# The PSUM pool of the down products in a decoder layer: two double banks, or four single ones

## The chip, the cores and the metric

The kernel runs on one core of a Trainium2 chip. The metric is the device time of one execution in microseconds. Five engines work from queues of their own: PE (TensorE, matmuls; its weight loads appear as PEld), DVE (VectorE, called V in the code), ACT (ScalarE, A), POOL (GpSimd, G) and SP (SyncE, which issues the DMAs here). Each takes its instructions in the order in which they stand in its queue, and engines wait for each other through semaphores. The sums of matmuls arise in PSUM; in this program a PSUM bank holds 512 f32 numbers for each of the 128 partitions, and eight banks are shared out by two pools.

## The reference, cut to what matters

The program is one whole decoder layer; the change lies in its second half, the feed-forward part, where 1024 tokens of width 1024 go through gate, up and down products with an inner width of 2816:

```python
def swiglu(h, w_gate, w_up, w_down):
    return (jax.nn.silu(h @ w_gate) * (h @ w_up)) @ w_down

h = x * (1.0 + scale2) + shift2
ffn = swiglu(h, w_gate[l], w_up[l], w_down[l])
x = layer_norm(ALPHA * x + gate2 * ffn, ln2_g[l], ln2_b[l])
```

## The kernel before

**Stages.** Modulation, projections, token index, attention and the output projection with the first layer norm take the first part of the program; the feed-forward part follows. It cuts the inner width of 2816 into 11 parts of 256 (`NFP`). For each part there is a gate product, an up product and a down product. All three use seven block products in place of eight (a Strassen scheme), with sums and differences of blocks; so a part has seven gate steps, seven up steps and seven down steps. In this text g0 to g6, u0 to u6 and d0 to d6 are these steps. For each part p from 1 to 9, the string `DOWN_AT` (L60) sets their order: g0 g1 d0 g2 d1 g3 d2 g4 d3 g5 d4 g6 d5 u0 d6 u1 u2 u3 u4 u5 u6, where the d steps belong to the part before. One such pass is called a round here. There are nine rounds; parts 9 and 10 get their down products after them, in the tail, by another loop.

**Steps.** A g or u step (`gu_step`, L1376) is 12 matmuls of 128x512 into one single bank of the pool `ps1` (u3 is cut in two halves of 6, the second behind u4). A d step (`down_step`, L1545) is also 12 matmuls: four groups of tokens, i = 0 to 3, with three matmuls each, into a bank for each group, b0 to b3. DVE then adds (or subtracts) each bank to a 512-wide half of a residual tile `res_X`, one instruction for each bank; these are called the reads of b0 to b3. Steps d0, d2, d4 and d6 begin a new sum (new tiles from the pool); d1, d3 and d5 add to the sum that stands in the bank, after DVE has read the partial sum once.

**PSUM before.** The pool `ps1` has four single banks, `ps2` has two tiles of two banks each. A new down sum takes both tiles of `ps2`: b0 and b1 are the halves of one, b2 and b3 of the other. The tile framework puts in the waits: a write to a tile waits for the reads of that tile that stand ahead of it in the program.

**Weights.** f32 precision is kept by splitting every operand in a rounded high part and a low rest, with three matmuls for a product. `make_block` (L1322) does it for a block of weights: where the scheme wants a sum or difference, POOL forms it in the raw weights first (`wraw`; for down weights POOL also multiplies by the gate); ACT writes the high half of the block (`wblk`, "the ACT half"); then DVE (gate and up) or POOL (down) writes the low half. There are four block buffers, and each step's end asks for the block that is needed four steps later, in the buffer that this step has just used. So on ACT, POOL and DVE the making of blocks stands in between the other work of the steps. Raw weights of a whole product (1 MB) have two buffers; the DMA for the next but one product is issued when the last block of a product is made.

**Order.** In the nine rounds PE, DVE, ACT and POOL run in the order of the program (`pinned`, L1564), with nothing reordered. After a g or u step's evacuation, the next lines of the program are the block (ACT half, DVE half), and then the d step with its reads. So DVE does the low half of a block for a gate or up step right ahead of the reads of the next d step.

The name `L159` in the profile is the helper through which all compute instructions go; the groups are told apart by their tiles: `gu` (gate and up sums), `dn` (down sums), `res_X`, `wblk`, `wraw`, `act` (activations split in two halves), `gtmp` and `utmp` (their intermediate sums).

Of the kernel before, what the change touches and what calls it, by code (L numbers as in the profile page):

```python
# [171 lines left out]
def decoder_layer_kernel(  # L172
# [16 lines left out]
        area[nm_] = at  # L189
        at += 4 * words  # L190
    nc.alloc_sbuf_tensor("arena", [P, (at - nc.sbuf_base) // 4], F32)
    ps2 = ctx.enter_context(tc.tile_pool(name="ps2", bufs=2, space=bass.MemoryType.PSUM))
    ps1 = ctx.enter_context(tc.tile_pool(name="ps1", bufs=4, space=bass.MemoryType.PSUM))

    def buf(where, off, n, name, dt=F32):
        return nc.alloc_sbuf_tensor_at(f"{name}_{where}{off}", [P, n], dt, offset=area[where] + 4 * off).ap()

    n_ps = [0]

    ps_ring = {"ps1": [], "ps2": []}  # L200

    def ps_tile(pool, tag, n, depth, nm):
        n_ps[0] += 1
        t = pool.tile([P, n], F32, tag=tag, name=f"{nm}_{n_ps[0]}")
        ring = ps_ring[tag]
        times.prev[t[:, 0:n].name] = ring[-depth] if len(ring) >= depth else None
        ring.append(t[:, 0:n].name)
        return t
# [4 lines left out]
    def psB(nm="pb"):  # L213
        return ps_tile(ps2, "ps2", 1024, 2, nm)
# [725 lines left out]
    for n_, (kind, a, b) in enumerate(groups):  # L940
        if n_ in PAIRS:
            pb = psB("pair")
# [184 lines left out]
    for n_, u in enumerate(units):  # L1127
        g, pr, i = u
# [178 lines left out]
    def block(n):  # L1307
        if n < 7:
            return FIRST[n]
        if n < len(blocks) - 8 or n >= len(blocks) - 4:  # L1310
            return RING[(n - 7) % NRING]
        return TOK[:, 1, n + 8 - len(blocks)]
# [50 lines left out]
    def use_blocks(n):  # L1363
        pos["used"] += n

        lead = LEAD + 4 if pos["used"] >= len(blocks) - 11 else LEAD
        while pos["made"] < min(pos["used"] + lead, len(blocks)):
            make_block()
# [76 lines left out]
    def after_step():  # L1445

        for f in low:
            f()
        low[:], low2[:] = low2, []

    def gate_up(kind, act, after=None):
        for n in range(7):
            gu_step(kind, n, 0, 4, act)
            if after is not None:
                after(n)
# [63 lines left out]
    def E(rc, i):  # L1519

        t = 7 - 2 * i if rc >= 20 else 6 - 2 * i
        return XR[t][:, 0:512] if rc % 10 == 1 else XR[t][:, 512:1024]
# [3 lines left out]
    def affine(n=0):  # L1526
        if todo:
            t = todo.pop(0)
            V.tensor_tensor(XR[t], XR[t], GR, ALU.mult)
            (G if t in AFF_G else V).tensor_tensor(XR[t], XR[t], lnb, ALU.add)  # L1530
            if t % 2 == 0:
                for to in (12, 21):
                    G.tensor_tensor(E(to, (7 - t) // 2), E(to, (7 - t) // 2), E(22, (7 - t) // 2), ALU.subtract)
            if not todo:
                SP.dma_start(GR, g2_d.to_broadcast([P, 1024]))
# [4 lines left out]
            affine()  # L1540
    gate_up("u", ACTS, lambda n: affine())

    bank = {}

    def down_step(p, n):  # L1545
        a_, w_, new, (to,) = DOWN[n]
        wd_ = block(pos["used"])
        if new:
            pb = [psB("dn"), psB("dn")]
            bank.update({i: pb[i // 2][:, (i % 2) * 512 : (i % 2 + 1) * 512] for i in range(4)})  # L1550
        for i in range(4):
            for m, (a, b) in enumerate(SPLITS):
                T.matmul(bank[i], ACTS[a_][:, a * 512 + i * P : a * 512 + (i + 1) * P], wd_[:, b * 512 : (b + 1) * 512],
                         start=(new and m == 0), stop=(m == 2), skip_group_check=True)
            z = E(abs(to), i)
            op = ALU.add if to > 0 else ALU.subtract
            if p == 0 and (n == 0 or not new):
                V.scalar_tensor_tensor(z, z, float(np.float32(ALPHA)), bank[i], ALU.mult, op)
            else:
                V.tensor_tensor(z, z, bank[i], op)  # L1560
        use_blocks(1)
        after_step()

    pinned.update("TVAG")  # L1564
    for p in range(1, NFP - 1):
        n_of = {"g": 0, "d": 0, "u": 0}
        for kind in DOWN_AT:
            n = n_of[kind]
            n_of[kind] += 1
            if kind == "d":  # L1570
                down_step(p - 1, n)
            else:
                gu_step(kind, n, 0, 4, None if kind == "g" else ACTS if p < NFP - 2 else PLAIN, kind == "u")
# [110 lines left out]
```

## Time and profile before

| | |
|---|---|
| median of 3 runs | 1800.81 us (1799.05 to 1803.73) |
| the profiled execution | 1800.09 us |
| its span on the engines | 1798.1 us, 15974 instructions |
| DVE busy | 1033.1 us (57%) |
| ACT busy | 607.8 us (34%) |
| POOL busy | 785.2 us (44%) |
| PE with d steps, by window | 106.0 us from 1056 to 1162: PE 71.82 us, DVE 40.32, ACT 22.05, POOL 38.03 busy |

How to read it: a row of the timeline gives the start of an instruction (or of a run of like ones) from the span's start, its duration, the engine, the operation with the tiles that it writes and reads, the count, and in brackets the idle time of the engine just before with what ended it. Rows of windows give the busy time of PE, PEld, DVE, ACT and POOL with counts in a stretch, the granted TensorE clock as a share of the full one, and the DMA's share and rate.

### The profile page before, as it was taken

The numbers are of one execution on the slowest core, as the hardware profiler recorded it, in microseconds if no ns is written. First come the engines' busy times: TensorE is split into PE (matmuls) and PEld (weight loads), VectorE is DVE, ScalarE is ACT, GpSimd is POOL, SyncE is SP. The second block draws the span as 40 slices with busy tenths as digits, with TensorE's granted clock in tenths as the row PEclk, the third lists the DMA queues.
The fourth block names the chain that finished last, engine by engine and source line by source line (L and its number), as shares of the span: only waits on it lengthen the run. The fifth ranks groups of instructions, "written<-read, shape, count | busy, mean of one in ns | idle before, by whom it ended". The sixth has DMA issues, their size and how long they took to land.

```text
span 1798.1 us, 15974 instructions
## 1 busy us (share of the span) xinstructions
PE 1348.8 (75%) x5462; PEld 1001.1 (56%) x5462; DVE 1033.1 (57%) x1740; ACT 607.8 (34%) x1141; POOL 785.2 (44%) x764
## 2 busy tenths in 40 slices
PE   8889786869979967676676857678576775766797
PEld 6655665645647866454454645456355553544576
DVE  7998989997784885333343333434333343333468
ACT  3556254656764552112121121212112122121231
POOL 1647576634453365615224161431614225162437
PEclk9999898878989988787886887878787797877999
DMA  9400120100464011010100101001010010101012
GB/s 352 165 36 30 53 101 17 59 18 13 146 224 153 1 36 59 0 47 24 47 24 24 47 1 47 23 24 47 1 47 24 24 47 9 61 2 47 24 71 94
DMA packets 24999, 101.80 MB, mean 57 GB/s; under 512 B 3411, under 2 KB 3411, under 8 KB 20566
## 3 DMA queue, kind: packets, MB, share of 16 engines
q1 hardware_dynamic: 24918, 100.78, 15.9%
q8 instruction: 43, 0.70, 0.2%
q14 instruction: 38, 0.31, 0.1%
HBM read 92.38 MB, written 8.40 MB: 56 GB/s over the span
## 4 chain that ended last, share of the span: by engine, by line
PE 29%; DVE 13%; POOL 7%; ACT 6%; issue 4%; DVEq 0%; ACTq 0%; POOLq 0%
PE gu L159 16%; PE dn L159 14%; DVE res_X L159 6%; POOL wraw_R L159 2%; DVE gtmp_V L159 2%; ACT wblk_V L159 2%; ACT wblk_T L159 2%; POOL wraw_W L159 1%; ACT gtmp_V L159 1%; POOL gtmp_V L159 1%; DVE wblk_V L159 1%; DVE wblk_T L159 1%; DVE act_W L159 1%; ACT act_W L159 1%; POOL act_W L159 1%
## 5 line engine op out<-in xcount | busy, mean ns | idle before, releaser
L159 DVE TENSOR_TENSOR res_X<-res_X,dn 128x512 f32<-128x512 f32 (+1 forms) x253 | 172.7, 683 | 179.9 <-PE dn L159 179.6
L159 PE MATMUL gu<-hr_H,wblk_V 128*128 128x512 f32 (+1 forms) x936 | 244.6, 417 | 18.0 <-POOL hr_H L159 11.7
L159 PE MATMUL gu<-hr_H,wblk_T 128*128 128x512 f32 (+1 forms) x924 | 247.3, 426 | 6.8 <-ACT gtmp_V L159 4.4
L159 PEld LDWEIGHTS gu<-hr_H,wblk_V 128*128 128x128 f32 x936 | 193.5, 211 | 62.2 <-POOL hr_H L159 12.3
L159 PE MATMUL dn<-wblk_V,act_W 128*128 128x512 f32 x324 | 122.5, 509 | 140.9 <-DVE res_X L159 123.8
L159 PEld LDWEIGHTS gu<-hr_H,wblk_T 128*128 128x128 f32 x924 | 197.4, 218 | 52.5 <-ACT gtmp_V L159 4.8
L159 PE MATMUL dn<-wblk_T,act_W 128*128 128x512 f32 x324 | 120.8, 504 | 136.8 <-DVE res_X L159 119.1
L159 PEld LDWEIGHTS dn<-wblk_V,act_W 128*128 128x128 f32 x324 | 70.7, 235 | 185.2 <-DVE res_X L159 152.7
L159 PEld LDWEIGHTS dn<-wblk_T,act_W 128*128 128x128 f32 x324 | 69.6, 231 | 180.1 <-DVE res_X L159 147.6
L159 POOL TENSOR_TENSOR wraw_R<-wraw_R 128x512 f32<-128x512 f32 x64 | 85.8, 1344 | 152.2 <-DVE wblk_V L159 81.2
L159 POOL TENSOR_TENSOR wraw_W<-wraw_W 128x512 f32<-128x512 f32 x60 | 78.6, 1315 | 135.1 <-DVE wblk_T L159 68.8
L159 PE MATMUL pj<-ws_W,hT_H 128*128 128x512 f32 x456 | 124.3, 421 | 17.8 <-ACT pout_K L159 5.4
L159 PEld LDWEIGHTS pj<-ws_W,hT_H 128*128 128x128 f32 x456 | 88.6, 201 | 45.4 <-issue 15.0
L159 ACT ACTIVATE wblk_V<-wraw_R 128x512 fp32r<-128x512 f32 x56 | 35.1, 627 | 166.0 <-PE dn L159 107.3
L159 POOL TENSOR_SCALAR sm_H<-sm_H,stat_X 128x1024 f32<-128x1024 f32 (+7 forms) x64 | 58.3, 924 | 71.2 <-DVE stat_X L159 58.2
L159 DVE TENSOR_TENSOR wblk_V<-wraw_W,wblk_V 128x512 fp32r<-128x512 f32 x40 | 31.2, 780 | 90.2 <-ACT wblk_V L159 89.8
L159 DVE TENSOR_TENSOR wblk_T<-wraw_W,wblk_T 128x512 fp32r<-128x512 f32 x41 | 31.3, 764 | 85.5 <-ACT wblk_T L159 85.3
L159 DVE TENSOR_TENSOR wblk_V<-wraw_R,wblk_V 128x512 fp32r<-128x512 f32 x38 | 29.8, 784 | 87.8 <-ACT wblk_V L159 84.3
L159 DVE TENSOR_SCALAR_CACHE_REDUCE junk_X<-keysD_T,colsD_X 128x1024 int16<-128x1024 int16 (+1 forms) x64 | 78.9, 1270 | 0.8
L159 ACT ACTIVATE wblk_T<-wraw_R 128x512 fp32r<-128x512 f32 x53 | 33.0, 625 | 128.3 <-PE dn L159 93.2
L159 ACT ACTIVATE wblk_T<-wraw_W 128x512 fp32r<-128x512 f32 x55 | 34.3, 625 | 123.0 <-PE dn L159 87.3
L159 ACT ACTIVATE wblk_V<-wraw_W 128x512 fp32r<-128x512 f32 x54 | 33.8, 626 | 124.0 <-PE dn L159 83.5
(299 smaller groups left out, 2805.4 us busy)
## 6 DMA issues: line engine op xcount, KB each, us to landing
wm_K<-in_wma_dram SPq DMA_DIRECT2D x16, 512.0 KB, 10.0
modraw_V<-in_wmc_dram SPq DMA_DIRECT2D x16, 512.0 KB, 4.3
wraw_R<-in_wg_dram SPq DMA_DIRECT2D x6, 1024.0 KB, 4.8
wraw_R<-in_wd_dram SPq DMA_DIRECT2D x6, 1024.0 KB, 4.8
wraw_W<-in_wup_dram SPq DMA_DIRECT2D x6, 1024.0 KB, 4.7
modraw_V<-in_wmg_dram SPq DMA_DIRECT2D x10, 512.0 KB, 4.6
wraw_R<-in_wup_dram SPq DMA_DIRECT2D x5, 1024.0 KB, 4.7
wraw_W<-in_wg_dram SPq DMA_DIRECT2D x5, 1024.0 KB, 4.8
```

The lines of the kernel that those rows point to most:

```text
L159: ins_ = f(*a, **k)
```

## The change

The pool of the double banks is closed when the last up product ahead of the rounds is written, and a third pool, `ps3`, of four single banks takes its place. A new down sum takes four single tiles of it. To let a pool be closed ahead of the others, `ps1` is now opened first, so the two pools lie the other way round in PSUM. Matmuls, reads, blocks, loads and their order are the same.

```diff
-    ps2 = ctx.enter_context(tc.tile_pool(name="ps2", bufs=2, space=bass.MemoryType.PSUM))
     ps1 = ctx.enter_context(tc.tile_pool(name="ps1", bufs=4, space=bass.MemoryType.PSUM))
+    pairs = ExitStack()
+    ps2 = pairs.enter_context(tc.tile_pool(name="ps2", bufs=2, space=bass.MemoryType.PSUM))
...
-    ps_ring = {"ps1": [], "ps2": []}
+    ps_ring = {"ps1": [], "ps2": [], "ps3": []}
...
     gate_up("u", ACTS, lambda n: affine())
 
+    pairs.close()
+    ps3 = ctx.enter_context(tc.tile_pool(name="ps3", bufs=4, space=bass.MemoryType.PSUM))
     bank = {}
 
     def down_step(p, n):
         a_, w_, new, (to,) = DOWN[n]
         wd_ = block(pos["used"])
         if new:
-            pb = [psB("dn"), psB("dn")]
-            bank.update({i: pb[i // 2][:, (i % 2) * 512 : (i % 2 + 1) * 512] for i in range(4)})
+            bank.update({i: ps_tile(ps3, "ps3", 512, 4, "dn") for i in range(4)})
```

On PE, the place is step d1 of the second round, where a sum that stands in the banks is added to. Before, `dn_5676` is the double bank of b0 and b1, and `dn_5677` that of b2 and b3:

```order
L159 MATMUL dn_5676<-wblk_V_4094,act_W_4105 128x512 [waits Activation_49]
L159 MATMUL dn_5676<-wblk_V_4094,act_W_4105 128x512 [waits Pool_49]
L159 MATMUL dn_5676<-wblk_V_4094,act_W_4105 128x512
L159 MATMUL dn_5676<-wblk_V_4094,act_W_4105 128x512 [waits DVE_49]
L159 MATMUL dn_5676<-wblk_V_4094,act_W_4105 128x512 x2
L159 MATMUL dn_5677<-wblk_V_4094,act_W_4105 128x512 x3
L159 MATMUL dn_5677<-wblk_V_4094,act_W_4105 128x512 [waits DVE_49]
L159 MATMUL dn_5677<-wblk_V_4094,act_W_4105 128x512 x2
```

The same step in the changed kernel, where `dn_5688` to `dn_5691` are the four single banks:

```order
L159 MATMUL dn_5688<-wblk_V_4094,act_W_4105 128x512 [waits DVE_49,Activation_49]
L159 MATMUL dn_5688<-wblk_V_4094,act_W_4105 128x512 [waits Pool_49]
L159 MATMUL dn_5688<-wblk_V_4094,act_W_4105 128x512
L159 MATMUL dn_5689<-wblk_V_4094,act_W_4105 128x512 [waits DVE_49]
L159 MATMUL dn_5689<-wblk_V_4094,act_W_4105 128x512 x2
L159 MATMUL dn_5690<-wblk_V_4094,act_W_4105 128x512 [waits DVE_49]
L159 MATMUL dn_5690<-wblk_V_4094,act_W_4105 128x512 x2
L159 MATMUL dn_5691<-wblk_V_4094,act_W_4105 128x512 [waits DVE_49]
L159 MATMUL dn_5691<-wblk_V_4094,act_W_4105 128x512 x2
```

Before, the write of b1 waits for DVE, and that of b3. Since both banks of a pair are one tile, the wait ahead of b1 is for the read of b0 in this same step. In the changed kernel each bank waits for DVE once, for the read of this bank in the step before; the waits for ACT and POOL (the block's two halves) are where they were.

On DVE, the order of instructions around the same step, before:

```order
L159 TENSOR_TENSOR wblk_T_4097<-wraw_R_4101,wblk_T_4097 128x512 [waits PE_49,Activation_49]
L159 TENSOR_TENSOR res_X_4079<-res_X_4079,dn_5676 128x512 [waits PE_49]
L159 TENSOR_TENSOR res_X_4077<-res_X_4077,dn_5676 128x512 [waits PE_49]
L159 TENSOR_TENSOR res_X_4075<-res_X_4075,dn_5677 128x512 [waits PE_49]
L159 TENSOR_TENSOR res_X_4073<-res_X_4073,dn_5677 128x512 [waits PE_49]
```

And in the changed kernel:

```order
L159 TENSOR_TENSOR wblk_T_4097<-wraw_R_4101,wblk_T_4097 128x512 [waits PE_49,Activation_49]
L159 TENSOR_TENSOR res_X_4079<-res_X_4079,dn_5688 128x512 [waits PE_49]
L159 TENSOR_TENSOR res_X_4077<-res_X_4077,dn_5689 128x512 [waits PE_49]
L159 TENSOR_TENSOR res_X_4075<-res_X_4075,dn_5690 128x512 [waits PE_49]
L159 TENSOR_TENSOR res_X_4073<-res_X_4073,dn_5691 128x512 [waits PE_49]
```

Nothing moved on DVE: the low half of the block still stands ahead of the four reads, and it waits for ACT. Only the tiles that the reads name are others.

## The prediction

> **What bounds the kernel now.** I read the page first (busy shares), then the list of waits, then the windows and the timeline of one round of the feed-forward part.
>
> ```profile
> PE 1348.8 (75%) x5462; PEld 1001.1 (56%) x5462; DVE 1033.1 (57%) x1740; ACT 607.8 (34%) x1141; POOL 785.2 (44%) x764
> PE dn L159 <- DVE res_X L159: 269.2, 126, 10.8
> ACT wblk_V L159 <- PE dn L159: 190.8, 32, 7.1
> ```
>
> No engine is full. The largest wait between PE and another engine is 269.2 us in 126 waits: a matmul of a down step waits for DVE to read a bank. Nine rounds of seven steps are 63 steps, so it is two waits a step: the writes of b1 and b3, which the order rows show waiting for the read of the other half of their pair. ACT in turn waits for PE to finish the step, since its block buffer is free only then. So the engines take turns.
>
> The windows show what this does to the clock, the timeline what it does to one step (d0 of the fifth round):
>
> ```profile
> 1166.50:1182.00 15.50, 12.04 (x33) 8.46 (x34) 4.73 (x7) 1.75 (x3) 9.62 (x8) 0.71 0.01 1
> 1132.00:1142.00 10.00, 10.00 (x46) 8.28 (x45) 3.93 (x6) 2.77 (x5) 0.00 (x0) 1.00 0.31 105
> 1165.78 0.67 DVE L159 TENSOR_TENSOR res_X<-res_X,dn 128x512 f32<-128x512 f32 x1
> 1166.51 2.93 PE L159 MATMUL dn<-wblk_V,act_W 128*128 128x512 f32 x6 [10.00 <-DVE res_X L159]
> 1168.20 0.69 DVE L159 TENSOR_TENSOR res_X<-res_X,dn 128x512 f32<-128x512 f32 x1 [1.74 <-PE dn L159]
> 1170.22 1.65 PE L159 MATMUL dn<-wblk_V,act_W 128*128 128x512 f32 x3 [0.78 <-DVE res_X L159]
> 1171.67 4.73 PE L159 MATMUL gu<-hr_H,wblk_T 128*128 128x512 f32 x12
> 1248.58 5.40 PEld L159 LDWEIGHTS gu<-hr_H,wblk_T 128*128 128x128 f32 x24
> ```
>
> PE stands 10.00 us before b1, until the read of b0 (1165.78) is done, writes b1 and b2 together, stands 0.78 us before b3. DVE in its turn waits 1.74 us for b1. Among these waits the granted clock is 0.71, and 12 matmuls take 4.73 us (0.39 us each); in the dense stretch of up steps it is 1.00, and 24 weight loads take 5.40 us (0.225 us for a load with its matmul).
>
> How long a round is, and where its up part ends, read from the first read of d0 (rounds 1, 6 and 9 here, round 5 above) and from ACT's copy of u4 (rounds 5 and 9), which starts when u4 is done:
>
> ```profile
> 733.14 0.68 DVE L159 SCALAR_TENSOR_TENSOR res_X<-res_X,dn 128x512 f32<-128x512 f32 x1
> 1275.25 0.67 DVE L159 TENSOR_TENSOR res_X<-res_X,dn 128x512 f32<-128x512 f32 x1
> 1599.27 0.67 DVE L159 TENSOR_TENSOR res_X<-res_X,dn 128x512 f32<-128x512 f32 x1
> 1247.64 0.60 ACT L159 ACTIVATE utmp_X<-gu 128x512 f32<-128x512 f32 x1 [2.96 <-PE gu L159]
> 1680.22 0.60 ACT L159 ACTIVATE utmp_X<-gu 128x512 f32<-128x512 f32 x1 [2.96 <-PE gu L159]
> ```
>
> Mean round: (1599.27 - 733.14) / 8 = **108.27 us**. In round 5 the part from d0's read to u4's end is 1247.64 - 1165.78 = 81.86 us, and from there to the next read of d0 27.61 us; in round 9 the first part is 80.95 us.
>
> **The change, part by part.** The two pools' places in PSUM, and closing one ahead of the rounds, add no instruction on any engine: nothing, and the stages ahead cost what they did. No matmul, read, block or DMA is added or moved. What goes are the 126 waits for the other half of a pair. What comes is a wait of each bank for its own read in the step before; a g or u step lies between. Behind a waiting matmul the whole PE queue stands, so ACT's copies of g and u steps and the release of block buffers do too. So I follow the reads of a round with the rows' durations, t counted from the first read of d0 in round 5:
>
> ```profile
> 1165.27 1.72 POOL L159 TENSOR_TENSOR act_W<-gtmp_V,act_W 128x512 fp32r<-128x512 f32 x1
> 1166.94 1.27 POOL L159 TENSOR_TENSOR wraw_R<-wraw_R,gr_G 128x512 f32<-128x512 f32 x1
> 1168.30 1.28 POOL L159 TENSOR_TENSOR wraw_R<-wraw_R 128x512 f32<-128x512 f32 x1
> 1171.96 0.63 ACT L159 ACTIVATE wblk_V<-wraw_R 128x512 fp32r<-128x512 f32 x1 [6.96 <-PE dn L159]
> 1172.67 1.27 POOL L159 TENSOR_TENSOR wblk_V<-wraw_R,wblk_V 128x512 fp32r<-128x512 f32 x1 [3.10 <-ACT wblk_V L159]
> 1173.91 1.27 POOL L159 TENSOR_TENSOR wraw_W<-wraw_W 128x512 f32<-128x512 f32 x1
> 1175.14 1.28 POOL L159 TENSOR_TENSOR wraw_R<-wraw_R,gr_G 128x512 f32<-128x512 f32 x1
> 1176.50 2.96 POOL L159 TENSOR_TENSOR wraw_R<-wraw_R 128x512 f32<-128x512 f32 x2
> 1177.63 0.69 DVE L159 TENSOR_TENSOR wblk_T<-wraw_W,wblk_T 128x512 fp32r<-128x512 f32 x1 [5.04 <-ACT wblk_T L159]
> 1178.24 0.68 DVE L159 TENSOR_TENSOR res_X<-res_X,dn 128x512 f32<-128x512 f32 x1
> 1184.43 1.29 POOL L159 TENSOR_TENSOR wraw_W<-wraw_W 128x512 f32<-128x512 f32 x1
> 1186.42 1.08 DVE L159 TENSOR_TENSOR wblk_V<-wraw_W,wblk_V 128x512 fp32r<-128x512 f32 x1 [3.31 <-ACT wblk_V L159]
> 1187.42 0.67 DVE L159 TENSOR_TENSOR res_X<-res_X,dn 128x512 f32<-128x512 f32 x1
> 1197.70 1.28 DVE L159 TENSOR_TENSOR gtmp_V<-gtmp_V,gu 128x512 f32<-128x512 f32 x2 [4.35 <-ACT gtmp_V L159]
> 1198.42 1.23 ACT L159 ACTIVATE gtmp_V<-gtmp_V 128x512 f32<-128x512 f32 x2 [0.75 <-DVE gtmp_V L159]
> 1200.81 0.68 DVE L159 TENSOR_TENSOR res_X<-res_X,dn 128x512 f32<-128x512 f32 x1
> 1200.96 0.33 SPq L156 DMA_DIRECT2D wraw_W<-in_wup_dram  x1
> wraw_W<-in_wup_dram SPq DMA_DIRECT2D x6, 1024.0 KB, 4.7
> 1212.22 0.68 DVE L159 TENSOR_TENSOR res_X<-res_X,dn 128x512 f32<-128x512 f32 x1
> 1222.82 0.68 DVE L159 TENSOR_TENSOR res_X<-res_X,dn 128x512 f32<-128x512 f32 x1
> 1232.74 0.68 DVE L159 TENSOR_TENSOR res_X<-res_X,dn 128x512 f32<-128x512 f32 x1
> ```
>
> - **d0 to d1** (12.46 us now). PE has long written all four banks, so the reads run from 0 to 2.8. Then POOL is late: its row of 1165.27 ends at t = 1.2, two operations on raw weights to 3.8, ACT half of d2's block 4.45 (its buffer is free now, so the 6.96 us wait goes), POOL's low half 5.75, the sum for g4's block 7.0, ACT half 7.7, DVE half 8.4. The reads of d1 start at **8.4**.
> - **d1 to d2** (9.18). POOL goes on from 7.0: gate and two differences for d3's block to 11.3, ACT half 11.9, low half 13.2, the difference for g5's block 14.5, ACT half 15.15, DVE half (1.08) 16.2. Reads of d2 at **16.2**.
> - **d2 to d3** (13.39). DVE's reads end at 19.0; two sums of g4's result to 20.3, ACT's two Silus to 20.95, ACT half of g6's block 21.55, DVE half 22.3. Reads of d3 at **22.3**.
> - **d3 to d4** (11.41). The DMA for the up weights is issued when g6's block is made, as now, but the first block from it comes sooner: 22.4 + 4.7 = 27.1, halves 27.7 and 28.4. Reads of d4 at **28.5**. Here a load that was hidden is seen.
> - **d4 to d6** (10.60 and 9.92). Reads of d4 end at 31.3; one sum, one Silu, u1's block: reads of d5 at **33.9** to 36.7; two DVE halves (u2, u3): reads of d6 at **38.1**.
> - **To u4's end** (14.90). PE may write d6 when DVE has read d5's b0, at 34.6. Behind it stand d6, u1, u2, half of u3 and u4: 54 matmuls x 0.225 = 12.2, so u4 ends at **46.8** in place of 81.86.
>
> PE has 24 matmuls for each pair of steps, 5.4 us at 0.225, in spacings of 5.4 to 8.4: it keeps up, at the full clock. From u4's end on, the 27.61 us are DVE, ACT and POOL working on u results, activations and blocks in turn; PE is not waited for, so I leave them whole. That is 74.4 us. DVE's halves that lie beside POOL's work took 1.08 in place of 0.69, and there will be more of this: three more of them, +1.2. A round comes to **75.6 us**, and the gain to 32.7.
>
> Sum: eight rounds x 32.7 = 261.4; the last one 80.95 - 48.0 = 32.9; together 294.3. The span of 1798.1 becomes 1503.8; the profiled execution lies 2.0 us above its span (1800.09), and 0.7 us below the median shown: **1506 us**.
>
> **The rivals.**
>
> *The clock stays low in the rounds.* For it: the window at 0.71 holds waits of only 0.78 us behind the long one, and the new order keeps short waits (PE is ahead of DVE at d2 to d5). Against it: dense stretches have 1.00, and PE would be far denser. If half the 174 matmuls from d1 to u4 took 0.39 (mean 0.31), PE would need 53.9 us from t = 0.7, so u4 ends at 54.6: a round 83.4, gain 8 x 24.9 + 25.1 = 224, **1576 us**. All at 0.39: 67.9 us, a round 97.4, about 1702.
> The Trainium skill ("TensorE: Matmul & The Clock Gate", section "A second HAM failure mode: psum-queue depth-cycling") speaks for this rival: cycling through PSUM banks lets PE idle briefly between groups, often enough that its clock gate swings. By that rule it is 1576; its section on oscillation names gaps above some 3.4 us, by which it is 1506, and the slow stretch behind waits of 0.78 us is not explained by that alone.
>
> *POOL becomes the bound.* If its nine operations between t = 1.2 and 14.5 all took the 1.72 us of its slow row, +3.9 us: a round 79.5, gain 259, **1541 us**. For it: DVE and POOL overlap more. Against: 1.28 (1168.30) stands beside a read of DVE already (1168.20).
>
> *It does not do what it says*: the tiles are separate, but another wait in the same place holds b1 and b3 back. The order rows show none. **1800 us.**
>
> *Slower*: DVE's read of a bank is held up while PE writes another. There are 28 reads a round; each would have to cost 32.7 / 28 = 1.17 us more (0.69 to 1.86) to use up the gain; at three times its length (2.07) a round is 114.2, **1854 us**. Against it: the read at 1168.20 took 0.69 while PE was writing b2 (1166.51 to 1169.44).
>
> **How the numbers follow.** Forecast 0.75, low clock 0.13, POOL 0.08, no effect 0.02, slower 0.02. The low end: without the +1.2, and with the up weights there in time (u0's DVE half right behind d3's reads, reads of d4 at 25.8 in place of 28.5), a round is 71.7, the gain 8 x 36.6 + 36.9 = 330: 1470. The high end takes in POOL and the half-slow clock: 1578. A measurement of this kernel can tell about 0.3% from no change; faster 0.96, same 0.02, slower 0.02.
>
> **What would show it.** The wait of dn for res_X falls from 126 waits, up to 10.8 us long, to one a step, mostly under 3 us; rounds of about 76 us between the first reads of d0; a step's four reads back to back; u0's ACT half waiting for a DMA; PEclk near 1.00 from d2 to u6, and 10 us of PE idle left at d0's end. It is wrong if the rounds' PEclk stays near 0.7 to 0.8, if the reads grow past 0.69, or if the 27.61 us stretch grows.

## The result and the profile after

| | before | after |
|---|---|---|
| median of the runs | 1802.27 us (1799.05 to 1804.48, 4 runs) | 1501.78 us (1499.32 to 1506.66, 4 runs) |
| the profiled execution, and its span | 1800.09 us, 1798.1 us | 1506.66 us, 1504.8 us |
| wait of `dn` for `res_X` on PE | 269.2 us, 126 times | 24.8 us, 14 times |
| mean round | 108.27 us | 75.07 us |

The changed kernel takes 0.8337 of the time before, with an interval of 0.8311 to 0.8363: some 300 us are gone.

The busy times on the page of the changed kernel:

```profile
PE 1267.5 (84%) x5462; PEld 974.9 (65%) x5462; DVE 1017.1 (68%) x1740; ACT 606.9 (40%) x1141; POOL 787.1 (52%) x764
```

The instructions are as many as before on every engine, and ACT and POOL were busy for as long as before. DVE's busy time fell by 16.0 us, and PE's by 81.3 us, from 1348.8 to 1267.5, with the same 5462 matmuls: 12 of them took 4.73 us before where the granted clock was 0.71, and take 2.88 us where it is 1.00, so part of the old "busy" was the low clock.

Its list of waits (engine, waiting tile, what it waits for; total, times, longest):

```profile
PE gu L159 <- ACT gtmp_V L159: 37.3, 13, 5.7
PE dn L159 <- DVE res_X L159: 24.8, 14, 2.6
```

The wait that was the longest of PE's is down to a tenth. The longest that PE still has for another engine in the rounds, 5.7 us, is for ACT's copy that frees a bank of a gate or up step. It comes once, in the first round; in the eight others this wait is 2.5 to 2.7 us, and 3.57 us for ACT's half of d0's block stand ahead of each of their d0 steps.

The same kernel's windows: the whole fifth round first, then its parts (columns: busy time of PE, PEld, DVE, ACT, POOL with their counts, granted clock, DMA share, GB/s).

```profile
1040.00:1115.30 75.30, 64.15 (x253) 50.82 (x252) 38.24 (x59) 22.28 (x38) 38.74 (x30) 0.91 0.12 42
1041.00:1057.00 16.00, 11.71 (x50) 8.95 (x49) 6.55 (x11) 4.11 (x7) 13.54 (x12) 1.00 0.00 0
1057.00:1062.00 5.00, 4.84 (x14) 3.87 (x15) 3.79 (x8) 2.00 (x5) 0.89 (x1) 0.66 0.00 0
1062.00:1088.00 26.00, 26.00 (x116) 21.54 (x115) 14.91 (x24) 7.82 (x14) 7.69 (x6) 1.00 0.29 97
1088.00:1115.30 27.30, 20.59 (x73) 15.66 (x72) 12.00 (x17) 8.34 (x15) 15.62 (x12) 0.83 0.06 24
```

The row of the whole round before reads:

```profile
1166.00:1275.00 109.00, 75.23 (x252) 54.78 (x252) 39.47 (x57) 22.37 (x38) 38.03 (x30) 0.80 0.09 29
```

The granted clock of a round rose from 0.80 to 0.91. From 1041 to 1057 POOL is the busiest engine (13.54 of 16 us); from 1062 to 1088 PE has no gap at all and sets the pace; behind that the old rest of 27 us follows, in which PE idles again. Between lies a stretch of 5 us at 0.66.

DVE's reads in the first, fifth and later rounds, on the timeline of the changed kernel (start, duration, count at the end):

```profile
739.96 2.47 DVE L159 SCALAR_TENSOR_TENSOR res_X<-res_X,dn 128x512 f32<-128x512 f32 x4
...
1039.94 2.47 DVE L159 TENSOR_TENSOR res_X<-res_X,dn 128x512 f32<-128x512 f32 x4
1048.76 2.47 DVE L159 TENSOR_TENSOR res_X<-res_X,dn 128x512 f32<-128x512 f32 x4
1056.33 2.47 DVE L159 TENSOR_TENSOR res_X<-res_X,dn 128x512 f32<-128x512 f32 x4
1061.82 2.47 DVE L159 TENSOR_TENSOR res_X<-res_X,dn 128x512 f32<-128x512 f32 x4
1068.04 2.47 DVE L159 TENSOR_TENSOR res_X<-res_X,dn 128x512 f32<-128x512 f32 x4
1072.94 2.48 DVE L159 TENSOR_TENSOR res_X<-res_X,dn 128x512 f32<-128x512 f32 x4
1077.13 2.47 DVE L159 TENSOR_TENSOR res_X<-res_X,dn 128x512 f32<-128x512 f32 x4
...
1115.29 2.47 DVE L159 TENSOR_TENSOR res_X<-res_X,dn 128x512 f32<-128x512 f32 x4
...
1340.53 2.47 DVE L159 TENSOR_TENSOR res_X<-res_X,dn 128x512 f32<-128x512 f32 x4
```

A step's four reads now stand back to back, x4 in 2.47 us, where before they came one by one with waits for PE between them. Eight rounds lie between 739.96 and 1340.53, so a round takes 75.07 us, and the rounds gain 8 x (108.27 - 75.07) = 265.6 us.

What is left to the end of the span from the ninth round's first read is 1798.1 - 1599.27 = 198.83 us before and 1504.8 - 1340.53 = 164.27 now: 34.6 us for the last round. The first read came at 733.14 before and 739.96 now, 6.8 us lost ahead of the rounds in this execution. 265.6 + 34.6 - 6.8 = 293.4, near the difference of the spans, 293.3.

### The profile page after: what moved, and what is told of

Same layout as the page of the kernel before. It is cut to its first block, busy times and chain, and to the rows that moved or that the text cites. A ratio compares the mean times of both kernels' runs of the same rounds, so it can differ in the third digit from the quotient of the medians.

```text
span 1504.8 us, 16018 instructions
## 1 busy us (share of the span) xinstructions
PE 1267.5 (84%) x5462; PEld 974.9 (65%) x5462; DVE 1017.1 (68%) x1740; ACT 606.9 (40%) x1141; POOL 787.1 (52%) x764
## 4 chain that ended last, share of the span: by engine, by line
PE 21%; POOL 16%; DVE 6%; ACT 4%; issue 3%; DMA 1%; DVEq 0%; POOLq 0%; ACTq 0%; SPq 0%
PE gu L159 11%; PE dn L159 9%; POOL wraw_R L159 5%; POOL wraw_W L159 4%; POOL act_W L159 2%; POOL gtmp_V L159 2%; DVE act_W L159 1%; DVE gtmp_V L159 1%; ACT wblk_T L159 1%; ACT wblk_V L159 1%; POOL wblk_T L159 1%; POOL wblk_V L159 1%; DVE utmp_X L159 1%; ACT act_W L159 1%; POOL res_X L159 1%
## 5 line engine op out<-in xcount | busy, mean ns | idle before, releaser
L159 PE MATMUL gu<-hr_H,wblk_V 128*128 128x512 f32 (+1 forms) x936 | 229.1, 397 | 28.7 <-ACT gtmp_V L159 16.7
L159 PE MATMUL gu<-hr_H,wblk_T 128*128 128x512 f32 (+1 forms) x924 | 228.3, 402 | 23.3 <-ACT gtmp_V L159 20.1
L159 PEld LDWEIGHTS gu<-hr_H,wblk_V 128*128 128x128 f32 x936 | 180.3, 197 | 69.8 <-ACT gtmp_V L159 20.0
L159 PEld LDWEIGHTS gu<-hr_H,wblk_T 128*128 128x128 f32 x924 | 180.5, 201 | 63.8 <-ACT gtmp_V L159 23.6
L159 DVE TENSOR_TENSOR res_X<-res_X,dn 128x512 f32<-128x512 f32 (+1 forms) x253 | 156.9, 676 | 1.8 <-PE dn L159 1.8
L159 PE MATMUL dn<-wblk_T,act_W 128*128 128x512 f32 x324 | 94.8, 447 | 23.7 <-ACT wblk_T L159 14.3
L159 PE MATMUL dn<-wblk_V,act_W 128*128 128x512 f32 x324 | 94.7, 447 | 22.8 <-ACT wblk_V L159 14.3
L159 DVE TENSOR_TENSOR wblk_T<-wraw_W,wblk_T 128x512 fp32r<-128x512 f32 x41 | 32.9, 805 | 76.8 <-ACT wblk_T L159 76.8
L159 DVE TENSOR_TENSOR wblk_T<-wraw_R,wblk_T 128x512 fp32r<-128x512 f32 x36 | 28.8, 805 | 64.2 <-ACT wblk_T L159 64.1
L159 ACT ACTIVATE wblk_V<-wraw_W 128x512 fp32r<-128x512 f32 x54 | 33.9, 627 | 79.3 <-POOL wraw_W L159 63.3
```

The costliest lines, as they stand in the source:

```text
L159: ins_ = f(*a, **k)
```

## The experiments

Ten runs in three groups, each compared with runs of the kernel before on the same chip (medians 1799.69, 1802.15 and 1803.85 us).

**One pair single, the other double.** Two theories stood against each other. In the rows of before, PE idles 10.00 us ahead of b1 and only 0.78 us ahead of b3. Either the wait of b1 is nearly the whole gain, or each pair alone holds PE and DVE in step. The first kernel makes only b0 and b1 single:

```diff
-    ps3 = ctx.enter_context(tc.tile_pool(name="ps3", bufs=4, space=bass.MemoryType.PSUM))
+    ps3 = ctx.enter_context(tc.tile_pool(name="ps3", bufs=2, space=bass.MemoryType.PSUM))
+    ps4 = ctx.enter_context(tc.tile_pool(name="ps4", bufs=1, space=bass.MemoryType.PSUM))
...
-            bank.update({i: ps_tile(ps3, "ps3", 512, 4, "dn") for i in range(4)})
+            pb = ps_tile(ps4, "ps4", 1024, 1, "dn")
+            bank.update({i: pb[:, (i % 2) * 512 : (i % 2 + 1) * 512] for i in (2, 3)})
+            bank.update({i: ps_tile(ps3, "ps3", 512, 2, "dn") for i in (0, 1)})
```

> The changed kernel with b0 and b1 in single banks, but b2 and b3 again the halves of one double bank: of the two waits a step, b1's is gone (the long one in the trace of before, up to 10.8 us) and b3's is back (0.78 us there). Theory A (a wait inside a step costs what PE then stands until DVE's reads of this step have come by, whichever bank has it): PE stops at b3 until DVE has read b2, 1.9 us after the step's first read starts, so the turn-taking is back; following a round with the rows, u4 ends at about 62 us after d0's first read in place of 47.7, a round is about 91, and the time 1645 us (1610 to 1700), less than half of the gain kept lost or more. Theory B (each wait is worth the idle time in its own row): only 63 waits of some 0.8 us come back, about 1550 us.

Measured: 1685.27 us, ratio 0.936 (0.9328 to 0.9392). The second kernel changes places: b2 and b3 single, b0 and b1 a double tile.

```diff
-            bank.update({i: pb[:, (i % 2) * 512 : (i % 2 + 1) * 512] for i in (2, 3)})
-            bank.update({i: ps_tile(ps3, "ps3", 512, 2, "dn") for i in (0, 1)})
+            bank.update({i: pb[:, (i % 2) * 512 : (i % 2 + 1) * 512] for i in (0, 1)})
+            bank.update({i: ps_tile(ps3, "ps3", 512, 2, "dn") for i in (2, 3)})
```

> The mirror: b0 and b1 the halves of one double bank, b2 and b3 single. b1's wait (the long one of before) is back, b3's is gone. Theory A: PE stands at b1 until DVE has read b0 (0.7 us after the first read starts) and then writes nine matmuls, so it is through 2.8 us after the first read starts, as in the other half-change (2.7): about the same time, 1645 us (1610 to 1700). Theory B: 269 - 63 x 0.78 = 220 us of waits stay, 1720 us or more, about 170 us over the other half-change.

Measured: 1714.68 us, ratio 0.9524 (0.9491 to 0.9556). From the kernel with b0 and b1 single, PE's total wait, and step d0 of a round on DVE's and on PE's timeline:

```profile
PE dn L159 <- DVE res_X L159: 200.2, 63, 10.6
```

```profile
1021.29 0.82 DVE L159 TENSOR_TENSOR wblk_T<-wraw_R,wblk_T 128x512 fp32r<-128x512 f32 x1 [5.31 <-ACT wblk_T L159]
1022.03 1.87 DVE L159 TENSOR_TENSOR res_X<-res_X,dn 128x512 f32<-128x512 f32 x3
1025.65 0.69 DVE L159 TENSOR_TENSOR res_X<-res_X,dn 128x512 f32<-128x512 f32 x1 [1.74 <-PE dn L159]
```

```profile
1023.96 1.65 PE L159 MATMUL dn<-wblk_V,act_W 128*128 128x512 f32 x3 [8.67 <-DVE res_X L159]
1025.41 4.89 PE L159 MATMUL gu<-hr_H,wblk_V 128*128 128x512 f32 x12
```

The wait ahead of b1 is gone, and one nearly as long, 8.67 us, stands ahead of b3 (1.7 to 3.6 us in the other steps of this round); the gate step behind it takes 4.89 us for 12 matmuls, against 2.88 at the full clock. The waits halved in number, from 126 to 63, but their total fell only from 269.2 to 200.2 us. The reason is on DVE's rows: its reads start late, behind the low half of the next block (1021.29). Whichever bank has to wait for a read of the same step waits for that moment. b3's 0.78 us in the rows of before (the same in all 63 steps, 49 us together) was short only because PE had already lost the time ahead of b1.

With only b0 and b1 double, the mirror image on PE:

```profile
PE dn L159 <- DVE res_X L159: 223.4, 63, 10.8
```

```profile
1028.92 3.69 PE L159 MATMUL dn<-wblk_V,act_W 128*128 128x512 f32 x9 [10.01 <-DVE res_X L159]
```

The two kernels are 29 us apart. By the rows of before they would have been some 170 apart, since the one removes the long wait and the other the short one: that theory falls, although its 1720 us or more for the second kernel, taken alone, is near what was measured. Nor do the halves add up. One pair alone gains some 115 us, the other some 85, both together 300: one remaining wait in a step is enough to keep PE in step with DVE for most of the gain. The other theory gave 1645 us for both; the first lies inside its range, the second 15 us above it. It had u4 end about 62 us after d0's first read; in the traces it is 67.9 and 71.3 us, and the stretch behind u4 is 27.6 to 27.7 us as before, so what it missed lies between d0 and u4. It reckoned with PE at the full clock, and the granted clock in a round was 0.86 and 0.83. That the clock accounts for the difference was not tried by itself.

**The place in PSUM.** The kernel before with the two pools opened in the new order and nothing else:

```diff
-    ps2 = ctx.enter_context(tc.tile_pool(name="ps2", bufs=2, space=bass.MemoryType.PSUM))
     ps1 = ctx.enter_context(tc.tile_pool(name="ps1", bufs=4, space=bass.MemoryType.PSUM))
+    ps2 = ctx.enter_context(tc.tile_pool(name="ps2", bufs=2, space=bass.MemoryType.PSUM))
```

> The kernel before with only the order of the two pools turned round, so that they lie in the other banks; pairs as before. My theory: where a pool lies costs nothing, and the 6.8 us by which d0's first read of the first round came later in the changed kernel's profile (739.96 against 733.14) are that execution's own: ratio 1.000, within 0.3%. Rival: the place costs the 6.8 us: 1809 us, ratio 1.004.

Measured: 1799.18 us, ratio 0.9992 (0.9977 to 1.0007). The other way round, the changed kernel with both pools in their old places until the rounds:

```diff
-    ps1 = ctx.enter_context(tc.tile_pool(name="ps1", bufs=4, space=bass.MemoryType.PSUM))
     pairs = ExitStack()
     ps2 = pairs.enter_context(tc.tile_pool(name="ps2", bufs=2, space=bass.MemoryType.PSUM))
+    pool1 = [pairs.enter_context(tc.tile_pool(name="ps1", bufs=4, space=bass.MemoryType.PSUM))]
...
     ps3 = ctx.enter_context(tc.tile_pool(name="ps3", bufs=4, space=bass.MemoryType.PSUM))
+    pool1[0] = ctx.enter_context(tc.tile_pool(name="ps1b", bufs=4, space=bass.MemoryType.PSUM))
```

> The changed kernel with the pools in the old places up to the rounds (double banks first; both pools are closed ahead of the rounds, four single banks for the down sums and four for gate and up opened in their place). My theory: as the changed kernel, 1502 us within 0.3%. Rival (the place costs 6.8 us of the head): 1495 us.

Measured: 1499.49 us, ratio 0.8328 (0.8308 to 0.8347). The place is worth nothing that can be measured (the interval of the swapped pools allows some 4 us), so the whole gain is the banks' tiles.

**The changed kernel once more**, unedited, to see whether the 6.8 us lost ahead of the rounds belong to the change.

> The changed kernel once more, on one chip with the two runs that follow, to put the loads' worth beside it. Ratio to before 0.833. Where the load reaches PE (0.5 to 0.7 us at d5, in the rounds in which d3 runs at the full clock) it should be worth at most 0.7 x 9 = 6 us.

Measured: 1501.3 us, ratio 0.8325 (0.8304 to 0.8346). A window ahead of the rounds, first in the profiled execution of the changed kernel, then in this one:

```profile
400.00:500.00 100.00, 97.60 (x560) 63.35 (x561) 74.20 (x161) 70.45 (x147) 40.24 (x42) 0.85 0.22 72
```

```profile
400.00:500.00 100.00, 93.92 (x585) 61.63 (x585) 77.72 (x170) 70.30 (x148) 42.31 (x43) 0.93 0.24 79
```

In the first execution the granted clock was 0.85 there and 560 matmuls were done in the 100 us; in the second it was 0.93, with 585. In the second the first read came at 734.93 instead of 739.96, so 5.0 of the 6.8 us went without any edit. In the profiles of the kernels tried, whatever the edit, it came between 732.55 and 737.61. So the lost 6.8 us are put down to that execution, not to the change.

**The load of the up weights.** The prediction had it come into view at d4. In four loads of 512 columns, the first quarter may start the block early:

```diff
-            SP.dma_start(raw_set(n), {"g": wg_in, "u": wup_in, "d": wd_in}[kind][p])
+            src = {"g": wg_in, "u": wup_in, "d": wd_in}[kind][p]
+            for q in range(4) if kind == "u" and 1 <= p < NFP - 1 else ():
+                SP.dma_start(raw_set(n)[:, q * 512 : (q + 1) * 512], src[:, q * 512 : (q + 1) * 512])
+            if not (kind == "u" and 1 <= p < NFP - 1):
+                SP.dma_start(raw_set(n), src)
```

> The changed kernel, but in the rounds the 1 MB load of the up weights is issued as four loads of 512 columns, so that u0's block waits for a quarter only. In the changed kernel's trace ACT stands 1.68 us there until the load has landed, as the prediction had it (a load that was hidden is seen). Theory of the prediction (d4's reads hang on the load, so the load is on the path): up to 1.7 us a round, 15 us in nine, 1487 us. Theory from the trace (PE runs without a gap from d3 to u6, so its matmuls set the end there and the wait lies beside them): no change, 1502 us within 0.3%.

Measured: 1494.16 us, ratio 0.8292 (0.8269 to 0.8315): between the two expectations. So it ran again beside the changed kernel on the same chip:

> The up weights in four loads, once more, now beside the changed kernel on one chip. Theory: 3 to 6 us under it (0.2 to 0.4%), since the wait at d5 goes in rounds at the full clock and lies beside a slow d3 in the others. Rival (it was the chip or the head's scatter): within 1 us of it.

Measured: 1494.21 us, ratio 0.8284 (0.8265 to 0.8303), and 7.1 us under the changed kernel's 1501.3, a little above what was expected. In the two profiled executions the spans are 8.0 us apart, but 2.4 of these lie ahead of the rounds (first reads at 734.93 and 732.55), which is the scatter that the rival named. From there to the ninth round's first read it is 600.25 us and 594.86 with the quarters: 5.4 us less, within the 3 to 6 expected. ACT in the changed kernel's fourth and fifth rounds, at the first block of the up weights:

```profile
992.19 0.63 ACT L159 ACTIVATE wblk_T<-wraw_R 128x512 fp32r<-128x512 f32 x1 [3.47 <-DMA wraw_R<-in_wup_dram]
...
1066.77 0.63 ACT L159 ACTIVATE wblk_V<-wraw_W 128x512 fp32r<-128x512 f32 x1 [1.68 <-DMA wraw_W<-in_wup_dram]
```

The load is seen, as predicted. But of its 3.47 us on ACT only 0.72 us reach PE in the fourth round, and none in the fifth, whose PE has no gap there (1062 to 1088 above):

```profile
994.30 2.97 PE L159 MATMUL dn<-wblk_T,act_W 128*128 128x512 f32 x12 [0.72 <-DVE res_X L159]
```

The rounds themselves show the same. Where d3 is slow, a round takes 75.3 to 75.4 us with either load; where it is not, 74.4 to 74.8 with the whole load and 73.7 to 73.8 with the quarters. So the quarters bring some 0.8 us in the rounds of the second kind, and nothing in those of the first. Of eight rounds, five were of the second kind in both executions traced with the quarters, and three in each of the three traced with the whole load (the changed kernel twice, and with the old places); why there are more is not shown. A wait on an engine that is not the bound was mostly covered here by the bound's own work.

**POOL in the first steps.** From 1041 to 1057 POOL was busy 13.54 of 16 us, and between the reads of d0 and d1 the blocks go through it one by one. Here three low halves a round, those of the blocks for d1, d2 and d3, go to DVE, which takes 0.69 us for one where POOL takes 1.29:

```diff
-        split(dst, src, 512, G if loads[n_set][0] == "d" and type(w_) is str else V)
+        split(dst, src, 512, G if loads[n_set][0] == "d" and w_ in ("B11", "T3", "B22", "T2") else V)
```

> The changed kernel with the low halves of the blocks for d1, d2 and d3 written by DVE in place of POOL (ahead of it DVE sits idle some 5 us twice). Theory (from u4's end to d3's start the round hangs on POOL's queue): two low halves of 1.29 us and two turns through ACT of about 0.7 us go from POOL's queue between d0's and d3's reads, and d1's half ahead of them: d3 starts 4 to 5 us sooner, 36 to 45 us in nine rounds, 1457 to 1466 us. Rival (DVE's queue takes it back, since the halves stand ahead of reads that PE waits for): 0 to 15 us, 1487 us or more.

Measured: 1463.08 us, ratio 0.812 (0.8098 to 0.8142). The reads of a round of this kernel on DVE:

```profile
945.64 2.47 DVE L159 TENSOR_TENSOR res_X<-res_X,dn 128x512 f32<-128x512 f32 x4
951.66 2.47 DVE L159 TENSOR_TENSOR res_X<-res_X,dn 128x512 f32<-128x512 f32 x4
957.68 2.47 DVE L159 TENSOR_TENSOR res_X<-res_X,dn 128x512 f32<-128x512 f32 x4
...
978.27 2.47 DVE L159 TENSOR_TENSOR res_X<-res_X,dn 128x512 f32<-128x512 f32 x4
1016.63 2.47 DVE L159 TENSOR_TENSOR res_X<-res_X,dn 128x512 f32<-128x512 f32 x4
```

d0's reads to d1's are 6.02 us (8.82 in the changed kernel), to d2's 12.04 (16.39), to d6's 32.63 (37.19). Of the 4.6 us gained there 4.4 stand to the next round: 70.99 us (75.35), and the time lies in the theory's range. So from d0 to d2 POOL set the pace of the changed kernel. PE's steps d2 and d3 of the same round:

```profile
952.48 2.97 PE L159 MATMUL dn<-wblk_V,act_R 128*128 128x512 f32 x12 [0.22 <-DVE res_X L159]
...
958.50 2.97 PE L159 MATMUL dn<-wblk_T,act_W 128*128 128x512 f32 x12 [0.33 <-DVE res_X L159]
```

Neither is slow here, and neither waits more than 0.33 us.

Next, two of POOL's sums for the activations' low halves go to DVE as well:

```diff
-ACT_G = ("S2", "S3", "S4")
+ACT_G = ("S4",)
```

> The one before, and the low halves of the activation sums S2 and S3 (1.27 us each on POOL, ahead of the gate for d1's block) on DVE as well, in its idle time ahead of d0's reads. Theory (the stretch from u4's end to d0's reads, 27.7 us, is POOL's queue too): d0's reads come about 2.2 us sooner, 20 us in nine rounds on top: about 1440 us (1432 to 1450). Rival (that stretch hangs on ACT and DVE): no more than the one before.

Measured: 1450.79 us, ratio 0.8049 (0.8028 to 0.8071): 12 us of the 20 or so hoped for, and just above the range expected. On POOL's timeline ahead of d0's reads in this kernel:

```profile
943.86 1.27 POOL L159 TENSOR_TENSOR act_W<-gtmp_V,act_W 128x512 fp32r<-128x512 f32 x1 [3.62 <-ACT act_W L159]
```

And on ACT's:

```profile
942.08 0.60 ACT L159 ACTIVATE gtmp_V<-gu 128x512 f32<-128x512 f32 x1 [1.39 <-DVE act_W L159]
```

The same copy on ACT in the changed kernel:

```profile
1036.25 0.60 ACT L159 ACTIVATE gtmp_V<-gu 128x512 f32<-128x512 f32 x1 [2.08 <-POOL act_W L159]
```

POOL now stands 3.62 us waiting for ACT, and ACT was itself held 1.39 us by DVE, which has the sums that POOL had, where POOL held it 2.08 us: the bound of this stretch has moved on. That the rest of the expected gain did not come for this reason fits these rows, but was not tried by itself.

Last, all three edits together:

> DVE writes the low halves of d1 to d3's blocks and of S2 and S3, and the up weights come in four loads. In the trace without the four loads PE stands 0.4 to 0.6 us at d5 in nearly every round, so they should be worth 0.4 to 0.7 us a round: 4 to 6 us under 1450.8, 1445 to 1447 us. Rival (what goes at d5 comes back as a wait at d6 or u0): 1451 us.

Measured: 1444.85 us, ratio 0.8009 (0.799 to 0.8029). That is just under the 1445 to 1447 us expected. It is the fastest kernel of this study, 56 us under the changed one's 1501.3.

## Why the prediction was right, point by point

**The time.** 1506 us were predicted, 1501.78 measured. The sum in the profiled executions was 294.3, the measured one 293.4. By terms: eight rounds 261.4 predicted and 265.6 measured, the last round 32.9 and 34.6, the pools' places and the head 0 and -6.8, of which the unedited rerun shows that they are no part of the change. Without that execution's head the gain is 300.2, so that 294.3 comes so near to 293.4 is partly luck: the forecast fell short by 5.9 us of gain, 4.2 of them in the eight rounds.

**The main step held**: the two waits of a step were for the other half of a pair, and taking them away lets PE run ahead of DVE. The experiments add that neither wait can be priced by itself.

**The reads, one by one** (us from d0's first read, fifth round):

| | d1 | d2 | d3 | d4 | d5 | d6 | u4's end |
|---|---|---|---|---|---|---|---|
| predicted | 8.4 | 16.2 | 22.3 | 28.5 | 33.9 | 38.1 | 46.8 |
| measured | 8.82 | 16.39 | 21.88 | 28.10 | 33.00 | 37.19 | 47.67 |

The chain through POOL to d1 and d2 is within 0.4 us. Its rows in the changed kernel (d0's reads, behind which the sums and halves follow as in the prediction's list):

```profile
1041.12 1.29 POOL L159 TENSOR_TENSOR wraw_R<-wraw_R,gr_G 128x512 f32<-128x512 f32 x1
1042.49 1.29 POOL L159 TENSOR_TENSOR wraw_R<-wraw_R 128x512 f32<-128x512 f32 x1
1043.82 0.63 ACT L159 ACTIVATE wblk_V<-wraw_R 128x512 fp32r<-128x512 f32 x1 [4.66 <-POOL wraw_R L159]
1044.53 1.29 POOL L159 TENSOR_TENSOR wblk_V<-wraw_R,wblk_V 128x512 fp32r<-128x512 f32 x1 [0.74 <-ACT wblk_V L159]
...
1047.76 1.08 DVE L159 TENSOR_TENSOR wblk_T<-wraw_W,wblk_T 128x512 fp32r<-128x512 f32 x1 [5.35 <-ACT wblk_T L159]
```

ACT's half at 1043.82 now waits for POOL, not for PE as before (6.96 us at 1171.96). DVE's half took 1.08 in place of 0.69, one of the three for which the 1.2 us were set aside.

**What was off is PE from d3 on.** The prediction had DVE's reads set the pace down to d6 and PE keep up at the full clock. On PE's timeline of the changed kernel, steps d2, d3, u0, d6 and what follows it:

```profile
1049.58 3.01 PE L159 MATMUL dn<-wblk_V,act_R 128*128 128x512 f32 x12 [2.59 <-DVE res_X L159]
1052.42 2.88 PE L159 MATMUL gu<-hr_H,wblk_T 128*128 128x512 f32 x12
1057.15 4.57 PE L159 MATMUL dn<-wblk_T,act_W 128*128 128x512 f32 x12 [1.85 <-ACT gtmp_V L159]
...
1072.45 2.88 PE L159 MATMUL gu<-hr_H,wblk_V 128*128 128x512 f32 x12
1075.17 2.88 PE L159 MATMUL dn<-wblk_V,act_W 128*128 128x512 f32 x12
1077.89 5.60 PE L159 MATMUL gu<-hr_H,wblk_T 128*128 128x512 f32 x24
```

d3 took 4.57 us at a granted clock of 0.66, d2 at the full clock 3.01. From 1057.15 on PE has no gap up to the end of the up steps, so its matmuls set the pace, and the reads of d5 and d6, although up to 0.9 us earlier than predicted, do not bring u4's end forward: d6 begins at 1075.17, t = 35.2, where 34.6 was predicted, and from there to u4's end it is 12.4 us instead of 12.2. The prediction's spacings "of 5.4 to 8.4" left out its own last one, 38.1 - 33.9 = 4.2 us from d5 to d6: by its own numbers PE had no time to spare there. The term that was mis-sized is "PE may write d6 when DVE has read d5's b0": PE was not waiting there. The 0.9 us by which u4's end was late is covered by the 1.2 us that stood for slow halves, which is luck rather than right reasoning.

**The stretch behind u4** is 1115.29 - 1087.61 = 27.68 us, from ACT's copy of u4 to the next read of d0 (27.61 predicted):

```profile
1087.61 0.60 ACT L159 ACTIVATE utmp_X<-gu 128x512 f32<-128x512 f32 x1 [2.96 <-PE gu L159]
```

**The marks that were named.** Four reads back to back, the load seen at u0's ACT half and a round of about 76 us were found. The clock was to be near 1.00 from d2 to u6; it was so but for the 5 us at d3 (at d2 in three of the nine rounds). The waits are fewer than one a step, 14 with a longest of 2.6 us (19 in the second execution), since from d3 on PE comes after the reads. The 10 us of PE's idle time at d0's end were not found; 6.7 us are left. On PE's timeline at the end of the fifth round:

```profile
1103.38 0.80 PE L159 MATMUL dn<-wblk_T,act_W 128*128 128x512 f32 x1 [3.57 <-ACT wblk_T L159]
1104.73 4.92 PE L159 MATMUL dn<-wblk_T,act_W 128*128 128x512 f32 x11 [0.56 <-POOL wblk_T L159]
1112.25 4.60 PE L159 MATMUL gu<-hr_H,wblk_T 128*128 128x512 f32 x12 [2.59 <-ACT gtmp_V L159]
```

PE waits 3.57 and 0.56 us for the two halves of d0's block and 2.59 us for a free bank behind it.

**The rivals.** The place was ruled out by two kernels. The reads did not slow down: four take 2.47, 0.62 each. POOL's operations between d0 and d2 kept their lengths (1.26 to 1.30 us, and the two differences 2.98 together, 2.96 before), so it did not become slower, though between d0 and d2 it is the bound, as the forecast's own chain had it. The rival of the low clock, with its 1576 us, stayed a small one: a few us of 0.66, in one place between d1 and u4. The Trainium skill ("TensorE: Matmul & The Clock Gate", section "A second HAM failure mode: psum-queue depth-cycling") speaks for it: in a kernel that cycles through PSUM banks PE idles briefly between groups of matmuls, often enough that its clock swings. As a forecast of the time it is not borne out here: the clock does swing once in that stretch, but PE cycles through four single banks in every step, and the granted clock of a round rose from 0.80 to 0.91.

## What to carry to other kernels

Where two banks are one tile, the framework has a write to the one wait for the read of the other; where the reading engine reaches its reads late in each step, that puts both engines in step, and one such wait a step is enough. So the idle time beside a wait is no price for it: to leave the one of 0.78 us a step, 49 us in the rows, cost 183 us here (1685.27 against 1501.78), and half of the cure brought about a third of the gain. Once the waits are gone, look stage by stage for the engine that is now last; here it was POOL for 16 us, then PE for 26 us, then the chain over ACT, DVE and POOL, and what was tried differs from stage to stage.

## What the runs showed of the chip

The granted clock fell behind pauses of PE shorter than the prediction had reckoned with. In the fifth round PE paused 2.59 us, worked 5.7 us at full clock, paused 1.85 us, and then had a granted clock of 0.66 for 5 us. In the fourth round the low piece came one step earlier:

```profile
974.83 4.24 PE L159 MATMUL dn<-wblk_V,act_R 128*128 128x512 f32 x12 [2.62 <-DVE res_X L159]
...
982.39 2.97 PE L159 MATMUL dn<-wblk_T,act_W 128*128 128x512 f32 x12 [0.21 <-DVE res_X L159]
```

There it falls on d2, in the stretch that POOL sets. That round began with this read on DVE:

```profile
965.17 2.47 DVE L159 TENSOR_TENSOR res_X<-res_X,dn 128x512 f32<-128x512 f32 x4
```

It took 1039.94 - 965.17 = 74.77 us; the fifth, with the low piece on d3, where PE has no gap to hide it in, took 75.35. Where the pauses were under 0.4 us, with three low halves on DVE, d2 and d3 both took 2.97. That these pauses cause the low clock is what the three cases fit with; it was not tried by itself, nor what share of busy time keeps the clock up. The length of a pause alone does not settle it: 2.6 us ahead of d2 were followed by a slow d2 in the fourth round and by a d2 at the full clock in the fifth. And in the first round of the second run with the quarter loads, pauses of 1.42 us ahead of d2 and 1.87 us ahead of d3 were followed by no slow step. The Trainium skill ("TensorE: Matmul & The Clock Gate", section "HAM oscillation — how this bites in real kernels") names idle gaps of more than some 3.4 us as what brings the clock down. Here the granted clock was 0.66 behind pauses of 2.59 and 1.85 us, so to stay under that figure is not enough.
